# Convolution taps, modulation and residual rows tied in order to the chunks of weights

## Chip, cores and metric

The kernel runs on one core of a Trainium2 chip. The metric is device time in microseconds (us) of one execution, as the median of three. PE is the matmul engine (TensorE), DVE the vector engine, ACT the scalar engine, POOL GpSimd, and SP the engine whose queue issues nearly all DMAs. Each engine works through its own instructions in program order and waits on semaphores for the others.

## What is computed

The program runs two blocks of two layers each, in float32. The first block takes x (256 tokens, width 1024) through windowed attention, a gated convolution and two MLPs. The second block, where most of the change lies, works on x and on 256 tokens of context:

```python
for l in range(DEPTH):
    with_ctx = l < DEPTH - 1
    sh1, sc1, g1, sh2, sc2, g2 = jnp.split((jax.nn.silu(c) @ w_mod[l] + b_mod[l])[:, None, :], 6, axis=-1)
    ...
    u = x * (1.0 + sc1) + sh1
    ...
    y, yc = token_mixer(u, uc, rope, w_in[l], ...)
    x = layer_norm(alpha * x + g1 * y, ln1_g[l], ln1_b[l])
    x = layer_norm(alpha * x + g2 * sq_relu_mlp(x * (1.0 + sc2) + sh2, ...), ln2_g[l], ln2_b[l])
```

The token mixer adds three branches under sigmoid gates: a depthwise convolution of 31 taps over 512 channels, an mLSTM in both directions with 4 heads, and a latent attention (MLA). In layer 1 only the 256 tokens of x are wanted at the end, so its queries, convolution and MLP cover those alone (tokens 256 to 511 in the kernel's numbering; 0 to 255 are the context).

## The kernel before

Every matrix product is done in split precision: an operand is cut into a high part and a low part, and three matmuls (high by high, L326; low by high, L327; high by low, L328) take the place of one. `w()` brings one 512 KB chunk of weights (8 tiles of 128x128): SP issues the DMA into `wr`, ACT copies it to the high part `wh` (L320), DVE subtracts for the low part `wl` (L321). `wr`, `wh` and `wl` have four buffers each, so a chunk's `wh` can't be written before the matmuls of the chunk four places earlier are done. One chunk feeds 24 matmuls, over 256 or 512 tokens.

Each engine's order is set ahead of time by a scheduler that plays the program through with priorities. Three devices steer it. `bg` holds generators that are stepped at marked places (`tick`). `queued()` puts a DMA behind the last DMA of weights. `behind()` gives all that it encloses a priority so low that it only fills gaps in the planned order.

Around the change:
- `conv()`: 120 taps of the convolution for each layer (30 taps by 4 channel tiles; L1061), each one DVE operation on 128x512 (layer 0) or 128x256 (layer 1), under `behind()`. They land among the work of the mLSTM heads.
- `mod(l)`: the modulation vectors from `w_mod`, as 48 DMAs of 512 KB (`mr`) with multiply-adds on DVE (`macd`, L842), then a small matmul (L850) and an addition (L854). `mod(1)` is stepped in `bg` during layer 0's MLP.
- `residual()`: alpha*x plus the row gate*bias for each token tile. The row is computed at full width on DVE (L890, L892: 128x1024), then applied (L900, L901: 128x1024).
- `ln()` normalises a token tile (statistics L954 and L955 on DVE, apply half on ACT L969, half on DVE L971). `make_u()` transposes it on PE (L932), applies the modulation (L937 on ACT, L939 on DVE) and splits it into `uh` (L388, ACT) and `ul` (L389, DVE).
- `ml_gates()`: a chain of operations on 36x512 (scans, copies, exponentials; L1112 to L1137) from the first two projection tiles `p1`, `p2` to the gates of the mLSTM, ending in two sets of transposes (L1145). `ml_project()` makes q, k, v, o of a head (`m_q` L1158 on ACT, `m_k` L1163 on DVE, `m_vt` L1168), and L1191 multiplies q by k.
- `tiles()` computes several projection tiles at once, by a list of parts (from k, to k, from token, to token).

## Time and profile before

| | us |
|---|---|
| median of 3 runs (2387.35 to 2390.11) | 2388.19 |
| the profiled execution's own time | 2387.22 |
| its span in the trace | 2385.2 |
| PE busy in the span | 2292.6 |
| DVE busy | 1722.4 |
| ACT busy | 1125.4 |

The span is the profiled time less 2.0 us around it. PE is busy 96% of it. The difference between span and PE's busy time, 92.6 us, is all the time in which PE had nothing to do; the mean granted clock of PE is 0.986 of full speed.

### The profile page before, as it was taken

To read this page: it belongs to the slowest core of one execution; us is meant where nothing else is said; L and a number is where in the kernel's file an instruction comes from. 1 tells how busy PE (TensorE), PEld (TensorE's weight loads), DVE (VectorE), ACT (ScalarE), POOL (GpSimd) and SP (SyncE) were. 2 spreads that over 40 slices of the span, in tenths; PEclk is the share of its full clock that TensorE was granted. 3 is DMA by queue.
4 is the path that set the end of the run, shared out by engine and by line. 5 is a ranking of instruction groups with operands and counts; after the bars stand their busy time and mean duration, and the time that the engine had idled before them with its cause. 6 is when DMAs were issued, how large, how long until landed. Compare 5 with 4: busy or idle time off the path is not lost.

```text
span 2385.2 us, 35271 instructions
## 1 busy us (share of the span) xinstructions
PE 2292.6 (96%) x13784; PEld 1966.7 (82%) x13796; DVE 1722.4 (72%) x2771; ACT 1125.4 (47%) x1718; POOL 64.1 (3%) x72
## 2 busy tenths in 40 slices
PE   8999989999999999999999999999998799998997
PEld 7888868888999888788777787777777699897996
DVE  6787877977666689956644477577788986857557
ACT  5555555554465444443442335343325355644653
POOL 1001100000000000000000000000000000000000
PEclk9999999999999999999999999999998899999999
DMA  5555546865655653222213343465544333345653
GB/s 198 205 188 175 191 134 204 263 217 185 188 177 187 189 175 106 76 78 65 88 54 115 100 148 132 142 194 180 178 140 138 109 108 115 133 152 185 202 186 114
DMA packets 120662, 364.62 MB, mean 153 GB/s; under 512 B 28528, under 2 KB 30320, under 8 KB 120496
## 3 DMA queue, kind: packets, MB, share of 16 engines
q1 hardware_dynamic: 120496, 362.38, 47.3%
q8 instruction: 108, 1.77, 0.3%
q14 instruction: 58, 0.48, 0.1%
HBM read 359.05 MB, written 3.28 MB: 152 GB/s over the span
## 4 chain that ended last, share of the span: by engine, by line
PE 87%; DVE 7%; DMA 3%; issue 1%; ACT 1%; SPq 0%; DVEq 0%; ACTq 0%
PE mm L326 26%; PE mm L327 26%; PE mm L328 26%; DMA mr<-in_w_mod 2%; DVE wl L321 2%; PE mm L1342 1%; PE tp L675 1%; PE mm L1356 1%; PE mm L1233 1%; DVE macd L842 1%; PE tp L850 1%; PE mm L561 1%; DVE cy L1061 1%; ACT wh L320 1%; PE mm L577 1%
## 5 line engine op out<-in xcount | busy, mean ns | idle before, releaser
L320 ACT CAST wh<-wr 128x1024 fp32r<-128x1024 f32 (+1 forms) x544 | 566.6, 1043 | 879.3 <-PE mm L327 491.7
L321 DVE TENSOR_TENSOR wl<-wr,wh 128x1024 fp32r<-128x1024 f32 (+1 forms) x544 | 658.7, 1213 | 361.4 <-ACT wh L320 351.2
L327 PE MATMUL mm<-ul,wh 128*128 128x256 f32 (+1 forms) x2224 | 709.2, 321 | 11.0 <-DVE ul L389 8.2
L328 PE MATMUL mm<-uh,wl 128*128 128x256 f32 (+1 forms) x2224 | 707.9, 320 | 2.9 <-DVE wl L321 2.9
L326 PE MATMUL mm<-uh,wh 128*128 128x256 f32 (+1 forms) x2224 | 703.8, 323 | 4.4 <-ACT m_q L1158 1.5
L327 PEld LDWEIGHTS mm<-ul,wh 128*128 128x128 f32 x2224 | 421.7, 190 | 45.2 <-DVE ul L389 9.2
L326 PEld LDWEIGHTS mm<-uh,wh 128*128 128x128 f32 x2224 | 415.9, 190 | 47.0 <-issue 5.4
L328 PEld LDWEIGHTS mm<-uh,wl 128*128 128x128 f32 x2224 | 421.2, 190 | 36.7 <-DVE wl L321 3.9
L842 DVE SCALAR_TENSOR_TENSOR macd<-mr,silu_c,macd 128x512 f32<-128x512 f32 x336 | 236.7, 745 | 40.0 <-DMA mr<-in_w_mod 30.9
L328 PE MATMUL mm<-wh,hl 128*128 128x512 f32 x640 | 252.4, 395 | 0.0
L327 PE MATMUL mm<-wl,hh 128*128 128x512 f32 x640 | 252.2, 395 | 0.0
L326 PE MATMUL mm<-wh,hh 128*128 128x512 f32 x640 | 251.1, 395 | 0.0
L326 PE MATMUL mm<-wh,uh 128*128 128x256 f32 x576 | 165.6, 291 | 3.0 <-ACT qk L532 2.3
L327 PE MATMUL mm<-wl,uh 128*128 128x256 f32 x576 | 164.7, 288 | 3.0 <-DVE wl L321 3.0
L328 PE MATMUL mm<-wh,ul 128*128 128x256 f32 x576 | 162.7, 285 | 0.1
L327 PEld LDWEIGHTS mm<-wl,hh 128*128 128x128 f32 x640 | 120.3, 188 | 30.6 <-DVE res L752 0.8
L326 PEld LDWEIGHTS mm<-wh,hh 128*128 128x128 f32 x640 | 120.2, 188 | 30.3 <-issue 2.5
L328 PEld LDWEIGHTS mm<-wh,hl 128*128 128x128 f32 x640 | 120.3, 188 | 28.7 <-issue 0.8
L1061 DVE SCALAR_TENSOR_TENSOR cy<-hpad,vecl,cy 128x512 f32<-128x512 f32 (+1 forms) x240 | 136.6, 606 | 0.1
L326 PEld LDWEIGHTS mm<-wh,uh 128*128 128x128 f32 x576 | 108.7, 190 | 8.3 <-ACT qk L532 3.3
L327 PEld LDWEIGHTS mm<-wl,uh 128*128 128x128 f32 x576 | 109.5, 191 | 7.2 <-DVE wl L321 4.0
L328 PEld LDWEIGHTS mm<-wh,ul 128*128 128x128 f32 x576 | 109.0, 190 | 0.7 <-DVE ul L422 0.3
(292 smaller groups left out, 2811.5 us busy)
## 6 DMA issues: line engine op xcount, KB each, us to landing
wr<-in_m SPq DMA_DIRECT2D x128, 512.0 KB
wr<-in_w SPq DMA_DIRECT2D x128, 512.0 KB
wr<-in_w_in SPq DMA_DIRECT2D x116, 512.0 KB
mr<-in_w_mod SPq DMA_DIRECT2D x96, 512.0 KB
...
```

Of the source, the lines that this page charges most:

```text
L320: nc.scalar.copy(hi[:, :n], raw[:, :n])
L321: nc.vector.tensor_tensor(lo[:, :n], raw[:, :n], hi[:, :n].bitcast(F32), ALU.subtract)
L326: mm(out, lh, rh, start=first, stop=False)
L327: mm(out, lh, rl, start=False, stop=False)
L328: mm(out, ll, rh, start=False, stop=last)
L561: mm(scs[hh][:, a:b], qT[hs, g, pr, qs], kT[hs, g, pr, :] if g == 0 else kT[hs, g, pr, qs], start=False, stop=g == 2)
L577: mm(po[hh * 64:hh * 64 + 64, qt * P:qt * P + P], v[:, j, g, h * 64:h * 64 + 64], pt[hh][:, blk * P:blk * P + P], start=blk == 0, stop=blk ...
L675: nc.tensor.transpose(tp[:, b * P:b * P + P], pm[:, b * P:b * P + P], self.ident)
L842: nc.vector.scalar_tensor_tensor(out=a, in0=raw[:, k], scalar=sc, in1=a, op0=ALU.mult, op1=ALU.add)
L850: nc.tensor.matmul(tp[q:q + 32, :], self.cst("ones")[:, 0:32], acc[:, half, v], start=True, stop=True, tile_position=(0, q))
L1061: nc.vector.scalar_tensor_tensor(out=ys[ft], in0=src, scalar=wk, in1=ys[ft], op0=ALU.mult, op1=ALU.add)
L1233: nc.tensor.matmul(pn[:, d * 130:d * 130 + 129], dts[d][:, s, i * P:i * P + P], v[:, s, 0:129], start=s == ks[0], stop=s == ks[-1])
```

## The change

A list `side` of generators is added. `w()` steps the first of them once after each chunk of weights when `side_n` is 1. What such a step issues stands under `pinned()`: its DMAs follow that chunk's DMA on SP, its ACT work follows that chunk's `wh`, its DVE work that chunk's `wl`. So the taps (6 per chunk in layer 0, 3 in layer 1), the modulation of both layers, and the residual rows have fixed places in each engine's order. `mod(1)` now begins after layer 0's MLA. The row gate*bias is computed once, in a layout of 128x8, by `bias_row()`, and kept in DRAM (`gbd`); the residual loads it ready-made. Layer 1 projects four tiles of the convolution for tokens 256 to 511 first, two k at a time (`BY_QUARTERS`), and the two gate tiles after them. The transposes at the end of the gate chain (`turn()`) come after head 0's projections in the program. Beside these, tiles are put into other pools, `row` has 5 buffers for 6, and layer 0's w_out input has its low half cut into pieces.

```diff
+BY_QUARTERS = tuple((k, k + 2, 256, 512) for k in range(0, 8, 2))
+TAPS = (6, 3)
...
-MT = ((1, 1), (5, 5), (0, 2))
+MT = ((1, 1), (5, 5), (0, 0))
...
+    def spin(self, n):
+        for _ in range(n):
+            if self.side:
+                try:
+                    next(self.side[0])
+                except StopIteration:
+                    self.side.pop(0)
+    def drain_side(self):
+        while self.side:
+            self.spin(1)
+    @contextmanager
+    def pinned(self):
+        with self.tc.issue_after(self.last_w), self.tc.issue_after(self.last_hi), self.tc.issue_after(self.last_lo):
+            yield
...
-        nc.scalar.copy(hi[:, :n], raw[:, :n])
-        nc.vector.tensor_tensor(lo[:, :n], raw[:, :n], hi[:, :n].bitcast(F32), ALU.subtract)
+        self.last_hi = nc.scalar.copy(hi[:, :n], raw[:, :n]).ins
+        self.last_lo = nc.vector.tensor_tensor(lo[:, :n], raw[:, :n], hi[:, :n].bitcast(F32), ALU.subtract).ins
+        self.spin(self.side_n)
...
+            if hc == 0 and bias is not None:
+                self.side_n = 1
...
-                    with self.queued():
+                    with self.pinned():
+                        raw = self.t(self.mp, [P, 2, 512], "mr", bufs=self.nmr)
                         nc.sync.dma_start(raw, self.A[f"w_mod_{l}"][sec * 2 + half, c])
...
+            if sec % 3 == 2:
+                with self.pinned():
+                    self.bias_row(l, sec // 3)
+                yield
...
+    def bias_row(self, l, sub):
+        nc = self.nc
+        row = lambda n: self.A["rows"][n].rearrange("(p k) -> p k", k=KT)
+        prev = l * 6 + 1 if sub else (l - 1) * 6 + 4
+        c = self.t(self.xp, [P, 4, KT], "brow")
+        nc.sync.dma_start(c[:, 2], row(l * 6 + sub * 3))
+        if prev > 0:
+            nc.sync.dma_start(c[:, 3], row(prev + 1))
+        for v in range(2):
+            nc.sync.dma_start(c[:, v], self.gdr[l][v, sub * 3 + 2, :].rearrange("(p k) -> p k", k=KT))
+        for v in range(2):
+            nc.vector.tensor_tensor(c[:, v], c[:, v], c[:, 2], ALU.mult)
+            if prev > 0:
+                nc.vector.scalar_tensor_tensor(out=c[:, v], in0=c[:, 3], scalar=ALPHA, in1=c[:, v], op0=ALU.mult, op1=ALU.add)
+            nc.sync.dma_start(self.gbd[l][v, sub, :].rearrange("(p k) -> p k", k=KT), c[:, v])
...
+    def residual_step(self, r, ag, gb):
+        e = self.nc.vector
+        if ag is None:
+            e.scalar_tensor_tensor(out=r, in0=r, scalar=ALPHA, in1=gb, op0=ALU.mult, op1=ALU.add)
+        else:
+            e.scalar_tensor_tensor(out=r, in0=r, scalar=ALPHA, in1=ag, op0=ALU.mult, op1=ALU.mult)
+            e.tensor_tensor(r, r, gb, ALU.add)
...
+    def residual(self, l, toks, G):
+        ss = sorted({j // 2 for j in toks})
+        with self.pinned():
+            ag = self.row(self.A["rows"][l * 6 + 1:l * 6 + 2])
+            gb = {s: self.row(self.gbd[l][1 - s:2 - s, 1, :]) for s in ss}
+        yield
+        for j in toks:
+            with self.pinned():
+                self.residual_step(self.res[j], ag, gb[j // 2])
...
-        with self.behind():
+        ys = [y[:, ft, :].rearrange("p (s t) -> p s t", s=ns) for ft in range(4)]
+        with self.pinned():
             for ft in range(4):
                 nc.scalar.activation(ys[ft], hp[ft][:, :, 0:256], AF.Identity, scale=self.vecl(f"w_dw_{l}", ft), bias=self.vecl(f"b_dw_{l}", ft))
-            for k in range(1, 31):
-                for ft in range(4):
+        yield
+        taps = [(k, ft) for k in range(1, 31) for ft in range(4)]
+        for a in range(0, 120, TAPS[l]):
+            with self.pinned():
+                for k, ft in taps[a:a + TAPS[l]]:
                     src, wk = hp[ft][:, :, k:k + 256], self.vecl(f"w_dw_{l}", k * 4 + ft)
                     nc.vector.scalar_tensor_tensor(out=ys[ft], in0=src, scalar=wk, in1=ys[ft], op0=ALU.mult, op1=ALU.add)
+            yield
...
+        def turn():
+            with self.tc.issue_after(self.last_mm):
+                for i, src in enumerate((an, li)):
+                    tp = self.ps("tp")
+                    for j in range(4):
+                        nc.tensor.transpose(tp[:, j * R:j * R + R], src[:, j * P:j * P + P], self.ident[0:R, 0:R])
+                    nc.vector.tensor_copy(cl[:, i], tp[:, 0:4 * R].rearrange("p (j r) -> p j r", j=4))
...
-                tis = [0, 1, T_CONV, T_CONV + 1]
-                p1, p2, *pre = self.tiles([A[f"w_in_{l}"][ti, 0] for ti in tis], uh, ul, 0, 512,
-                                           ((0, KT, 0, 256), (0, KT, 256, 512)) if l == 0 else
-                                           ((0, KT, 256, 512), (0, KT, 0, 256, (0, 1))))
-                if l:
-                    pre = [p_[:, 256:512] for p_ in pre]
+                first = lambda tis, c0, parts: self.tiles([A[f"w_in_{l}"][ti, 0] for ti in tis], uh, ul, c0, 512, parts)
+                hp, pre = [], []
+                conv_in = self.conv_in(l, xg, uh, ul, pre, hp)
+                if l == 0:
+                    p1, p2, *more = first([0, 1, T_CONV, T_CONV + 1], 0, ((0, KT, 0, 256), *BY_QUARTERS))
+                    pre += more
+                else:
+                    pre += first(range(T_CONV, T_CONV + 4), 256, BY_QUARTERS)
+                    next(conv_in)
+                    p1, p2 = first([0, 1], 0, ((0, KT, 256, 512), (0, KT, 0, 256)))
...
-                self.conv(l, self.conv_in(l, xg, uh, ul, pre), cy)
+                self.run(conv_in)
+            self.side, self.side_n = [self.conv(l, hp, cy)] + ([self.residual_x()] if l else []), 1
...
+            gates[2]()
...
         if l == 0:
+            self.drain_side()
             hx.close()
...
                 o = self.mla(l, xo, v, ks, qs, cq[0][2])
+                if l == 0:
+                    self.mp, self.nmr = self.cm.enter_context(tc.tile_pool(name="mod1", bufs=1, side="right")), 2
+                    self.side.append(self.mod(1))
...
-            with self.behind():
-                G = self.residual(l, 1, toks, l * 6 + 1)
+            G = {}
+            self.side.insert(0, self.residual(l, toks, G))
...
-                     ((0, KT, 256, 512), (0, KT, 0, 256)) if l == 0 else ((0, KT, 256, 512),), MT[2], ready)
-            self.drain_bg()
+                     (*BY_QUARTERS, (0, KT, 0, 256)) if l == 0 else BY_QUARTERS, MT[2], ready)
+            self.side_n = 0
```

What this makes of the engines' orders is shown at three places. The numbers at a tile's end tell one buffer from another.

First, DVE at the start of layer 0's MLP, while PE waits for `ul`. Before, in the middle of it:

```order
L939 TENSOR_SCALAR mt_13618<-tp_13613,aff_a_13241,aff_b_13242 128x256
L939 TENSOR_SCALAR mt_13628<-tp_13623,aff_a_13241,aff_b_13242 128x256
L890 TENSOR_TENSOR row_13666<-row_13664,row_13658 128x1024
L842 SCALAR_TENSOR_TENSOR macd_13993<-mr_14074,silu_c_83,macd_13993 128x512 x2
L389 TENSOR_TENSOR ul_13240<-mt_13618,uh_13239 128x2x256
L900 SCALAR_TENSOR_TENSOR resb_2291_13210<-resb_2291_13210,row_13660 128x1024
L900 SCALAR_TENSOR_TENSOR resb_2292_13211<-resb_2292_13211,row_13660 128x1024
L389 TENSOR_TENSOR ul_13240<-mt_13628,uh_13239 128x2x256
L892 SCALAR_TENSOR_TENSOR row_13666<-row_13662,row_13666 128x1024
L842 SCALAR_TENSOR_TENSOR macd_13993<-mr_14074,silu_c_83,macd_13993 128x512 x2
L939 TENSOR_SCALAR mt_13638<-tp_13633,aff_a_13241,aff_b_13242 128x256
L890 TENSOR_TENSOR row_13675<-row_13673,row_13658 128x1024
```

After, from the last four `mt` on (L998 and L413 are the former L939 and L389, L344 the former L321, L931 the former L900):

```order
L998 TENSOR_SCALAR mt_13768<-tp_13763,aff_a_13391,aff_b_13392 128x256
L998 TENSOR_SCALAR mt_13778<-tp_13773,aff_a_13391,aff_b_13392 128x256
L413 TENSOR_TENSOR ul_13390<-mt_13768,uh_13389 128x2x256
L413 TENSOR_TENSOR ul_13390<-mt_13778,uh_13389 128x2x256
L998 TENSOR_SCALAR mt_13788<-tp_13783,aff_a_13391,aff_b_13392 128x256
L998 TENSOR_SCALAR mt_13798<-tp_13793,aff_a_13391,aff_b_13392 128x256
L413 TENSOR_TENSOR ul_13390<-mt_13788,uh_13389 128x2x256
L413 TENSOR_TENSOR ul_13390<-mt_13798,uh_13389 128x2x256
L344 TENSOR_TENSOR wl_14054<-wr_14051,wh_14053 128x1024
L344 TENSOR_TENSOR wl_14090<-wr_14087,wh_14089 128x1024
L931 SCALAR_TENSOR_TENSOR resb_2314_13359<-resb_2314_13359,row_14057 128x1024
```

The full-width rows L890, L892, L900, L901 and the `macd` no longer stand between `mt` and `ul`; the residual follows after two chunks' `wl`.

Second, DVE at the end of layer 0's MLP, where the statistics of token tiles 2 and 3 (`resb` ..93 and ..94, the first to be normalised) are made. Before, these rows stand between the last additions of the tiles and their statistics' end:

```order
L321 TENSOR_TENSOR wl_16624<-wr_16621,wh_16623 128x1024
L1574 TENSOR_TENSOR tl_16311<-mm_16229,row_13673 128x512
L954 BN_STATS bst_16359<-resb_2294_13213 128x6
L1577 TENSOR_TENSOR resb_2293_13212<-resb_2293_13212,tl_16308 128x512
L1577 TENSOR_TENSOR resb_2294_13213<-resb_2294_13213,tl_16311 128x512
L321 TENSOR_TENSOR wl_16655<-wr_16652,wh_16654 128x1024
L954 BN_STATS bst_16347<-resb_2293_13212 128x6
L1574 TENSOR_TENSOR tl_16461<-mm_16409,row_13664 128x512
L954 BN_STATS bst_16359<-resb_2294_13213 128x6
L1574 TENSOR_TENSOR tl_16464<-mm_16410,row_13664 128x512
L321 TENSOR_TENSOR wl_16686<-wr_16683,wh_16685 128x1024
L955 BN_AGGR bmv_16345<-bst_16347 128x2
```

After (L1658 and L1661 are the former L1574 and L1577, L1013 and L1014 the former L954 and L955, L1030 the former L971; tiles 2 and 3 are `resb` ..16 and ..17):

```order
L1658 TENSOR_TENSOR tl_16362<-mm_16282,row_14240 128x512
L1661 TENSOR_TENSOR resb_2316_13361<-resb_2316_13361,tl_16362 128x512
L1658 TENSOR_TENSOR tl_16365<-mm_16283,row_14240 128x512
L1013 BN_STATS bst_16382<-resb_2316_13361 128x6
L1661 TENSOR_TENSOR resb_2317_13362<-resb_2317_13362,tl_16365 128x512
L1014 BN_AGGR bmv_16380<-bst_16382 128x2
L1013 BN_STATS bst_16394<-resb_2317_13362 128x6
L387 TENSOR_SCALAR brs_16381<-bmv_16380 128x1
L1014 BN_AGGR bmv_16392<-bst_16394 128x2
L387 TENSOR_SCALAR brs_16393<-bmv_16392 128x1
L1024 TENSOR_SCALAR bmr_16388<-bmv_16380,brs_16381 128x1
L1030 TENSOR_SCALAR resb_2316_13361<-resb_2316_13361,bmv_16380,brs_16381 128x512
```

The `wl` of the next chunks and the `tl` of the other two token tiles have moved behind the normalisation of tiles 2 and 3.

Third, DVE in layer 1 ahead of head 0's `m_k`, for which q by k waits. After:

```order
L1198 COPY g_z_16863<-g_li_16862 4x512
L1122 SCALAR_TENSOR_TENSOR cy_16585<-hpad_16742,vecl_16368,cy_16585 128x256
L1198 COPY g_l_16870<-g_u_16869 4x512
L344 TENSOR_TENSOR wl_17366<-wr_17363,wh_17365 128x1024
L1122 SCALAR_TENSOR_TENSOR cy_16585<-hpad_16993,vecl_16368,cy_16585 128x256
L1122 SCALAR_TENSOR_TENSOR cy_16585<-hpad_17028,vecl_16368,cy_16585 128x256
L1122 SCALAR_TENSOR_TENSOR cy_16585<-hpad_16738,vecl_16368,cy_16585 128x256
L1199 COPY g_li_16862<-g_2863_16860 36x512
L1267 TENSOR_TENSOR g_t_17221<-g_m_17219,trir_16592 128x256
L1200 COPY g_li_16862<-g_2863_16860 4x512
L1229 TENSOR_SCALAR m_k_17080<-mm_17079,vecl_16368 128x512
```

And PE there: before, the gates' transposes L1145 stand ahead of q by k (L1191):

```order
L328 MATMUL mm_17264<-uh_16343,wl_17269 128x256
L1145 MATMUL tp_16801<-cst_65,g_z_16769 128x36 x4
L1145 MATMUL tp_16807<-cst_65,g_li_16768 128x36 x4
L1171 MATMUL tp_17258<-cst_65,m_vt_17226 128x128 x4
L1191 MATMUL mm_17299<-m_q_17160,m_k_17193 128x256
```

After, q by k (L1257) follows the last projection, and the transposes (L1211) follow it:

```order
L352 MATMUL mm_17157<-uh_16378,wl_17162 128x256
L1257 MATMUL mm_17207<-m_q_17043,m_k_17080 128x256
L1257 MATMUL mm_17210<-m_q_17043,m_k_17080 128x256
L1257 MATMUL mm_17213<-m_q_17043,m_k_17080 128x256
L1257 MATMUL mm_17216<-m_q_17043,m_k_17080 128x256
L1237 MATMUL tp_17151<-cst_65,m_vt_17116 128x128 x4
L1211 MATMUL tp_17194<-cst_65,g_z_16863 128x36 x4
```

The gates' transposes have moved behind q by k. `m_k` stands on DVE behind `wl_17366`, the low part of a chunk of head 1 that is four chunks after the one (`wl_17162`) that the last projection of head 0 reads; before, too, it stood behind the `wl` of that chunk, and behind the gate chain.

## Rows read from the trace of the kernel before

**Rows 1.** The page's part 1: busy time, share of the span, instructions.

```profile
PE 2292.6 (96%) x13784; PEld 1966.7 (82%) x13796; DVE 1722.4 (72%) x2771; ACT 1125.4 (47%) x1718; POOL 64.1 (3%) x72
```

**Rows 2.** Waits of PE: line, what ended it, us in total, times, longest.

```profile
PE tp L932 <- ACT resb L969: 17.0, 3, 9.3
PE mm L327 <- DVE ul L389: 8.2, 5, 4.4
```

**Rows 3.** Windows: length; busy PE, PEld, DVE, ACT, POOL; granted clock; DMA share; GB/s.

```profile
0.00:800.00 800.00, 769.32 (x5437) 690.84 (x5450) 600.62 (x862) 434.83 (x656) 39.02 (x24) 0.99 0.60 193
870.00:1010.00 140.00, 137.80 (x658) 110.97 (x658) 138.02 (x261) 56.97 (x109) 3.03 (x4) 1.00 0.30 95
2170.00:2200.00 30.00, 21.81 (x126) 19.21 (x126) 21.45 (x34) 10.75 (x15) 1.29 (x2) 0.83 0.56 193
```

**Rows 4.** Two windows in layer 0's MLP start, columns as in rows 3.

```profile
1440.00:1445.00 5.00, 1.10 (x8) 0.69 (x6) 5.00 (x7) 1.24 (x2) 0.00 (x0) 0.86 0.00 0
1445.00:1450.00 5.00, 3.58 (x16) 3.58 (x17) 5.00 (x8) 0.00 (x0) 0.00 (x0) 0.50 0.00 0
```

**Rows 5.** DVE timeline there: start, us, line, operation, idle before and releaser.

```profile
1440.50 1.22 DVE L890 TENSOR_TENSOR row<-row,row 128x1024 f32<-128x1024 f32 x1
1441.64 0.54 DVE L939 TENSOR_SCALAR mt<-tp,aff_a,aff_b 128x256 f32<-128x256 f32 x1
1442.09 2.35 DVE L901 TENSOR_TENSOR resb<-resb,row 128x1024 f32<-128x1024 f32 x2
1444.36 1.41 DVE L842 SCALAR_TENSOR_TENSOR macd<-mr,silu_c,macd 128x512 f32<-128x512 f32 x2
1445.68 0.69 DVE L389 TENSOR_TENSOR ul<-mt,uh 128x512 fp32r<-128x512 f32 x1
```

**Rows 6.** PE timeline, end of layer 0's MLP and start of layer 1.

```profile
1799.54 0.40 PE L328 MATMUL mm<-wh,hl 128*128 128x512 f32 x1
1809.28 0.69 PE L932 MATMUL tp<-cst,resb 128*128 128x128 f32 x2 [9.34 <-ACT resb L969]
...
1815.23 0.41 PE L327 MATMUL mm<-ul,wh 128*128 128x256 f32 x1
...
1823.54 0.39 PE L327 MATMUL mm<-ul,wh 128*128 128x256 f32 x1 [1.36 <-DVE ul L389]
```

**Rows 7.** DVE timeline at the same boundary.

```profile
1790.94 0.69 DVE L854 SCALAR_TENSOR_TENSOR mt<-tp,mt 128x512 f32<-128x512 f32 x1 [2.61 <-PE tp L850]
...
1803.18 1.22 DVE L321 TENSOR_TENSOR wl<-wr,wh 128x1024 fp32r<-128x1024 f32 x1
```

**Rows 8.** PE timeline, layer 1, last projection of head 0 to q by k.

```profile
1866.51 0.29 PE L326 MATMUL mm<-uh,wh 128*128 128x256 f32 x1
...
1869.28 0.29 PE L328 MATMUL mm<-uh,wl 128*128 128x256 f32 x1
1876.77 0.64 PE L1145 MATMUL tp<-cst,g_z 36*128 36x36 f32 x4 [7.21 <-DVE g_z L1135]
1881.62 0.64 PE L1145 MATMUL tp<-cst,g_li 36*128 36x36 f32 x4 [4.21 <-DVE g_li L1137]
1883.50 1.08 PE L1171 MATMUL tp<-cst,m_vt 128*128 128x128 f32 x4 [1.24 <-ACT m_vt L1168]
1884.87 3.22 PE L1191 MATMUL mm<-m_q,m_k 128*128 128x256 f32 x8 [0.28 <-DVE m_k L1163]
...
1939.72 1.89 PE L1191 MATMUL mm<-m_q,m_k 128*128 128x256 f32 x8
```

**Rows 9.** DVE groups by form: count, busy us, mean ns, idle before.

```profile
L1061 DVE SCALAR_TENSOR_TENSOR cy<-hpad,vecl,cy 128x512 f32<-128x512 f32 x120 | 84.8, 740 | 0.0
L1061 DVE SCALAR_TENSOR_TENSOR cy<-hpad,vecl,cy 128x256 f32<-128x256 f32 x120 | 51.8, 473 | 0.1
```

**Rows 10.** Waits of DVE, columns as in rows 2.

```profile
DVE wl L321 <- ACT wh L320: 351.2, 255, 5.5
DVE macd L842 <- DMA mr<-in_w_mod: 30.9, 23, 3.7
```

155 lines of the change are left out of this document (76 added, 79 removed).

## Prediction

> **What bounds the kernel now.** First the busy times: PE works for 2292.6 of 2385.2 us [rows 1], so whatever the change does to DVE, ACT or the DMAs, it pays only through the 92.6 us in which PE stands idle, or through PE's clock. The same number of matmuls is issued before and after. Next, the waits of PE, to see who owns that idle time: the largest entry is the transposes of `make_u` behind the layer norm (17.0 us in three waits), then matmuls behind `ul` (8.2 us in five) [rows 2]. Last, the timelines at those places. Three stretches hold what the change can touch.
>
> Place A is the start of layer 0's MLP. Two windows of 5 us have PE busy 1.10 and 3.58 us, the second at a granted clock of 0.50, the lower of the two levels (1.2 of 2.4 GHz) [rows 4]. DVE is full there and does other things between `mt` and `ul`: a row (1.22), two residual additions (2.35), two `macd` (1.41) [rows 5].
>
> Place B is the boundary of the layers. The last matmul of the MLP ends at 1799.94; PE then idles 9.34 us, and the first matmul that needs `ul` starts at 1815.23, 15.3 us after that end; another 1.36 us are lost at 1823.54 [rows 6]. DVE reached this late: it had stood 2.61 us at the end of the modulation (L854), and `wl` of later chunks ran among the statistics [rows 7].
>
> Place C is layer 1's first head. Its last projection (24 matmuls, 1866.51 to 1869.57) is followed by waits of 7.21, 4.21, 1.24 and 0.28 us, for the end of the gate chain above all. q by k starts at 1884.87, 15.3 us after the projection's end, and runs 3.22 us, where the same eight elsewhere take 1.89 [rows 8].
>
> **The change part by part.** *A.* The rows, additions and `macd` leave the space between `mt` and `ul`, which becomes 0.54+0.54 and 0.69+0.69 us of DVE work a pair. PE's two windows were 10 us with 4.68 busy: 5.3 us idle, which is to go; of the 3.58 busy at half clock, half, 1.8 us, comes back with it [rows 4]. That is 7.1. A little more is in the other waits for `ul`: the 8.2 less the longest (4.4) less B's 1.36 is 2.4 over three places [rows 2, 6], of which I take 0.5 here: **7.5 us**, from 5.3 (the clock falls anyway, since the layer norm just ahead stays) to 9.5.
>
> *B.* The program now normalises token tiles 2 and 3 without `wl` among the statistics, and without the modulation's end, so that the first transposes come before the MLP's last eight matmuls. After the last matmul DVE has still to do, ahead of the first `ul`: a `tl` and an addition of the last tiles, a statistic (each 512 wide, near 0.69 like the `ul` [rows 5]), a `wl` (1.22 [rows 7]), two `mt` (1.08), another addition, and the `ul` itself: 5 x 0.69 + 1.22 + 1.08 = 5.75 us. So the first `ul` is late by 5.8 us where it was by 15.3: 9.5 us. The following `ul` come every 3 us at most and feed quarters of 24 matmuls, 2.9 to 3.1 us each (24 matmuls of 256 columns, [rows 8]), so 1.36 goes too, less half a us for order: **10 us**, from 7 (layer norm as late as ACT and DVE can make it) to 11.
>
> *C.* The work from the boundary to the end of head 0's last projection is the same; conv tiles go first. What then gates q by k is `m_k`. On DVE it stands behind the `wl` of a chunk whose `wh` buffer is the one that the last projection reads. So after that projection's end come, in series: `wh` on ACT (about 1.05, bounded by the `wl` of the same size, 1.22 [rows 7]), `wl` (1.22), three taps (0.42 each by their pace, 0.47 by their mean [rows 9]), three short copies (0.4 each), `m_k` (0.74, the size of a tap of 512 [rows 9]): 1.05+1.22+1.35+1.2+0.74 = 5.6 us. That is the new wait, in place of 15.3; but the transposes of gates and v (0.64+0.64+1.08 = 2.36 at low clock, about 1.2 at full [rows 8]) were within the 15.3 and now follow q by k as work. 15.3-5.6-1.2 = **8.5 us**, from 4 to 14 (no wait at all, and q by k back to 1.89). The gate chain has to end some 19 us (10+8.5) earlier than it did, with four conv tiles ahead of it and fewer taps between its steps; the sum holds if it ends by `m_k`.
>
> Here a rule speaks against the change. Every matmul, `m_k` and `wl` in the rows ran in the order of its program: nothing overtook `m_q` or `m_k` in the 15.3 us [rows 8]. The Trainium skill, in "TensorE: Matmul & The Clock Gate", section "Architectural detail: the array is 16× 32×32, not 1× 128×128", states that ScalarE and VectorE take their queues strictly first in, first out, and that PE pulls only weight loads ahead. By it C keeps the new wait, and tying work to chunks lengthens every queue behind a late chunk; were it not so, C would give 5.6 us more. The trace agrees with the rule.
>
> *D.* Layer 1's MLP start: 8.2 us of 30 idle [rows 3], 7.2 of it the layer norm's latency (17.0 less 9.34 and small change [rows 2, 6]). That chain is not shortened. The row's load and 0.6 us of `ul` waits go: **1 us**, 0 to 2.
>
> *Modulation in the first block.* The same 124 `macd` and the same DMAs, now at fixed places. Its waits for `mr` (30.9 us in 23, [rows 10]) stand on DVE; PE waits little for weights, and has 30.7 us idle in 800 for all causes [rows 3]. Each waiting `macd` now holds the next chunk's `wl`; four buffers, some 12 us of matmuls at 256 columns, cover the longest wait, 3.7. I take 0, from +3 to -6 (two longest waits reaching PE).
>
> *Layer 0's taps and heads.* 120 taps at 84.8 us [rows 9] in a stretch where DVE is busy 138.02 of 140 and PE 137.80 [rows 3]. Six per chunk spread them over 20 chunks; the load is the same and has no reserve. 0, from +2 to -8.
>
> *The rest.* Six rows and four additions less at 1.22 [rows 5] take 12 us off DVE, mostly in A and B, counted there. `bias_row` adds some 14 operations of 128x8, bounded from below by nothing and from above by 0.54 (a 128x256 [rows 5]): 0 to 7.6 us on a DVE that idles 28% of the span [rows 1], and not on the path. `mod(1)`, 48 portions of four `macd`, 3 us each by 1.41 for two, stands beside MLP chunks of twice 2.9 us: hidden; without that cover each portion would cost its 3 us. 0, +-2.
>
> Sum: 7.5+10+8.5+1 = 27 us. Against the profiled execution's own 2387.2 that is 2360.2; the median of the runs shown is 1.0 above the profiled one, so the forecast is **2361 us**.
>
> **The rivals.** *Less at C.* The gate chain, steps on DVE and ACT in turn, starts later behind conv tiles and is cut by taps, so that it is late again and holds q by k (through ACT, where `m_q` follows its last exponential) or the transposes just behind. For it: it was the longest wait, 7.21+4.21 [rows 8]. Against it: fewer taps stand between its steps. C then gives 0 and the sum is 18.5: about 2370.
>
> *More.* The queues come through without the wait at C and without low clock: 5.6+1.3 us more, and 3 in the first block: about 2351.
>
> *Slower: the tied portions starve the weights.* A `wl` waits for its `wh` 1.38 us on average (351.2 in 255, [rows 10]); now this idle time is filled by taps that may run at any time. Tied taps can't fill it, since they stand behind that very `wl`. If that is paid ahead of each of layer 0's 20 portions and ten of layer 1's 40, it is 41 us where DVE has 2 us of reserve [rows 3]: 2361+41 = 2402. It decides from 20 such portions on, 27 us. Against it: `wl` waits because it is early, four chunks ahead; a DVE that is behind doesn't wait for `wh`. By the Trainium skill's rule above, first in, first out, this is what would happen wherever `wh` itself is late.
>
> *No effect.* The layer norm's latency rules B as it does D, A is held by the same latency, and C's wait only moves: gains of 3 to 5 us and as much lost in the heads: 2387.
>
> **How the numbers follow.** A measurement here can tell about 0.2%, 4.8 us, from no change. Forecast 0.60 (2354 to 2368 by its own bounds), less at C 0.16, more 0.10, slower 0.08, no effect 0.06. Faster by over 0.2% (under 2383.4): the first three, 0.86; same 0.06; slower 0.08. The range leaves out the last two and a little of the case "more": 2348 to 2380.
>
> **What would show it.** Right: in the window of place A PE busy throughout and clock 1.00; at the boundary an idle gap of about 6 us in place of 9.34 and later waits; a wait of PE of 5 to 6 us for `m_k` or `m_q` behind the last projection, and none of over 2 us for the gates; `macd` gone from the layer 0 MLP's end. Wrong: DVE waiting on `wh` between portions of taps with PE waiting for `wl` in the heads of layer 0 (about 870 to 1010), `macd` waits that show up on PE in the first block, or a gate chain that ends after `m_k`.

## The result and the profile after

The changed kernel takes 2359.68 us (median of four runs, 2358.84 to 2359.88) where the kernel before takes 2387.77: a ratio of 0.9881 with a 95% interval of 0.9864 to 0.9898, or 28 us less. The profiled execution has a span of 2357.0 us, 28.2 less than before. The forecast was 2361 us.

The page's part 1 shows something that the forecast did not have. This is the row that answers to [rows 1]:

```profile
PE 2273.7 (96%) x13784; PEld 1965.6 (83%) x13796; DVE 1710.3 (73%) x2779; ACT 1126.6 (48%) x1718; POOL 69.0 (3%) x72
```

PE issues the same 13784 instructions, but its busy time fell by 18.9 us, from 2292.6. Its idle time, the only thing that the prediction counted on, fell by 9.3 us alone (from 92.6 to 2357.0 - 2273.7 = 83.3). So two things have to be explained: where two thirds of the gain come from, and why the idle time that was predicted to go by 27 went by 9.

The waits of PE show where the idle time now stands (us in total, times, longest), against [rows 2]:

```profile
PE mm L1257 <- DMA g_m<-g_md: 7.7, 1, 7.7
PE tp L991 <- ACT resb L1028: 7.2, 1, 7.2
PE mm L1134 <- DVE mt L1132: 7.2, 1, 7.2
PE tp L441 <- DMA x<-in_x_p: 6.1, 1, 6.1
PE mm L409 <- ACT l_h L412: 6.1, 1, 6.1
PE tp L991 <- DVE mt L998: 5.2, 3, 3.3
...
PE mm L1257 <- ACT m_st L1258: 2.8, 4, 1.0
```

The 17.0 us behind the layer norm are down to 7.2 (place D, which stays). The gates' 7.2 and 4.2 are gone, and a 7.7 has come at q by k (L1257), near the forecast's 5 to 6. Two long waits are new: L409, in layer 1's latents, and L1134, the convolution's norm.

Windows of the changed kernel (length; busy PE, PEld, DVE, ACT, POOL; granted clock of PE; DMA share; GB/s):

```profile
0.00:800.00 800.00, 776.93 (x5523) 698.06 (x5536) 607.50 (x873) 441.77 (x662) 40.24 (x25) 0.99 0.60 197
870.00:1010.00 140.00, 134.16 (x643) 107.66 (x641) 136.84 (x269) 61.32 (x124) 3.02 (x4) 1.00 0.29 94
1400.00:1455.00 55.00, 51.93 (x334) 46.77 (x334) 40.21 (x53) 32.57 (x44) 2.16 (x2) 1.00 0.48 163
1600.00:1700.00 100.00, 100.00 (x448) 80.95 (x447) 66.15 (x88) 34.56 (x38) 0.00 (x0) 1.00 0.45 145
1900.00:2060.00 160.00, 144.30 (x1009) 128.88 (x1007) 129.76 (x293) 80.06 (x145) 6.41 (x5) 0.95 0.35 113
```

The first 800 us hold 7.6 us more of busy PE than in [rows 3]. Place A now lies within 1400 to 1455 and keeps its full clock, where [rows 4] had 0.86 and 0.50. The last window, layer 1's latents and the convolution's norm, is the worst: 15.7 of 160 us idle.

The timeline of PE at the boundary, at q by k of layer 1's first head, and at the two new waits:

```profile
1766.25 0.38 PE L991 MATMUL tp<-cst,resb 128*128 128x128 f32 x2
...
1768.10 0.39 PE L352 MATMUL mm<-wh,hl 128*128 128x512 f32 x1
1768.33 0.82 PE L991 MATMUL tp<-cst,resb 128*128 128x128 f32 x6
1772.44 1.82 PE L991 MATMUL tp<-cst,resb 128*128 128x128 f32 x8 [3.29 <-DVE mt L998]
...
1774.91 0.41 PE L351 MATMUL mm<-ul,wh 128*128 128x256 f32 x1
...
1827.77 0.28 PE L352 MATMUL mm<-uh,wl 128*128 128x256 f32 x1
1835.71 3.75 PE L1257 MATMUL mm<-m_q,m_k 128*128 128x256 f32 x8 [7.66 <-DMA g_m<-g_md]
...
1954.59 1.84 PE L409 MATMUL mm<-cst,l_a 128*128 128x1 f32 x8 [6.09 <-ACT l_h L412]
...
2018.20 1.22 PE L1134 MATMUL mm<-mt,cst 128*128 128x256 f32 x2 [7.17 <-DVE mt L1132]
```

At the boundary the first two transposes run between the MLP's last matmuls, as the order said they could, and the first `ul` matmul starts 6.4 us after the MLP's end (1768.49 to 1774.91) where it was 15.3 [rows 6]. At q by k the releaser named, a DMA of `g_m`, is not an operand of the matmul; `m_k` and `m_q` are. DVE ends `m_k` at 1835.40, 0.3 us before, and ACT ends `m_q` at 1835.16, after an idle time that ended with L1200, the last operation of the gate chain on DVE:

```profile
1834.69 0.47 ACT L1224 ACTIVATE m_q<-mm,vecl 128x256 f32<-128x256 f32 x1 [5.64 <-DVE g_li L1200]
```

The timeline of DVE ahead of it:

```profile
1831.09 1.23 DVE L344 TENSOR_TENSOR wl<-wr,wh 128x1024 fp32r<-128x1024 f32 x1
1832.23 1.27 DVE L1122 SCALAR_TENSOR_TENSOR cy<-hpad,vecl,cy 128x256 f32<-128x256 f32 x3
1833.42 0.41 DVE L1199 COPY g_li<-g 36x512 f32<-36x512 f32 x1
1833.75 0.41 DVE L1267 TENSOR_TENSOR g_t<-g_m,trir 128x256 f32<-128x256 f32 x1
1834.20 0.42 DVE L1200 COPY g_li<-g 4x512 f32<-4x512 f32 x1
1834.65 0.75 DVE L1229 TENSOR_SCALAR m_k<-mm,vecl 128x512 f32<-128x512 f32 x1
```

From its `wl` on, that is the series of the prediction (a `wl`, three taps, three short operations, `m_k`), and it is dense: nothing in it waits for `wh`. ACT had ended the `wh` of that `wl` at 1829.05, 2.0 us before DVE came to it.

### The profile page after: what moved, and what is told of

Its sections match the earlier page's. It is cut to its first block, busy times and chain, and to the rows that moved or that the text cites. A ratio compares the mean times of both kernels' runs of the same rounds, so it can differ in the third digit from the quotient of the medians.

```text
span 2357.0 us, 35325 instructions
## 1 busy us (share of the span) xinstructions
PE 2273.7 (96%) x13784; PEld 1965.6 (83%) x13796; DVE 1710.3 (73%) x2779; ACT 1126.6 (48%) x1718; POOL 69.0 (3%) x72
## 4 chain that ended last, share of the span: by engine, by line
PE 52%; DVE 4%; ACT 1%; issue 1%; DMA 0%; POOL 0%; DVEq 0%; ACTq 0%; POOLq 0%
PE mm L350 16%; PE mm L351 15%; PE mm L352 15%; PE mm L1408 1%; DVE wl L344 1%; PE mm L1422 1%; PE mm L1299 1%; PE tp L699 1%; DVE cy L1122 1%; PE mm L1257 1%; PE tp L877 0%; PE tp L991 0%; ACT wh L343 0%; DVE bst L1013 0%; DVE tl L1658 0%
## 5 line engine op out<-in xcount | busy, mean ns | idle before, releaser
L344 DVE TENSOR_TENSOR wl<-wr,wh 128x1024 fp32r<-128x1024 f32 (+1 forms) x544 | 659.7, 1215 | 343.2 <-ACT wh L343 337.6
L352 PE MATMUL mm<-uh,wl 128*128 128x256 f32 (+1 forms) x2224 | 704.8, 319 | 2.7 <-DVE wl L344 2.7
L350 PE MATMUL mm<-uh,wh 128*128 128x256 f32 (+1 forms) x2224 | 701.3, 321 | 4.1 <-ACT m_q L1224 1.5
L350 PEld LDWEIGHTS mm<-uh,wh 128*128 128x128 f32 x2224 | 417.8, 191 | 42.4 <-ACT wh L343 5.0
L352 PEld LDWEIGHTS mm<-uh,wl 128*128 128x128 f32 x2224 | 422.7, 190 | 34.6 <-DVE wl L344 3.7
L352 PE MATMUL mm<-wh,hl 128*128 128x512 f32 x640 | 249.2, 391 | 0.0
L350 PE MATMUL mm<-wh,hh 128*128 128x512 f32 x640 | 247.5, 391 | 0.0
L350 PE MATMUL mm<-wh,uh 128*128 128x256 f32 x576 | 165.4, 291 | 2.6 <-ACT qk L556 1.5
L352 PE MATMUL mm<-wh,ul 128*128 128x256 f32 x576 | 162.9, 285 | 0.1
L350 PEld LDWEIGHTS mm<-wh,hh 128*128 128x128 f32 x640 | 120.0, 188 | 28.3 <-issue 3.4
L352 PEld LDWEIGHTS mm<-wh,hl 128*128 128x128 f32 x640 | 120.1, 188 | 26.7 <-issue 0.8
L350 PEld LDWEIGHTS mm<-wh,uh 128*128 128x128 f32 x576 | 108.4, 190 | 9.6 <-issue 4.6
L352 PEld LDWEIGHTS mm<-wh,ul 128*128 128x128 f32 x576 | 109.0, 190 | 0.7 <-DVE ul L446 0.3
```

What stands on the lines that cost most here:

```text
L344: self.last_lo = nc.vector.tensor_tensor(lo[:, :n], raw[:, :n], hi[:, :n].bitcast(F32), ALU.subtract).ins
L350: mm(out, lh, rh, start=first, stop=False)
L352: self.last_mm = mm(out, ll, rh, start=False, stop=last).ins
```

## Where the 28 us lie, stage by stage

The 11,760 matmuls of the projections (L326 to L328, now L350 to L352) are the same in number in all versions. Numbered in the order in which they start, the start of the same number in two traces says how far one is ahead, and the difference over a stage what the stage gives. Two pairs of kernels are compared, each with its big operands at the same places in SBUF (why that matters is the first experiment): the change against `before_m128`, and `pad128` against the kernel before. Negative is faster, in us.

| stage | after - before_m128 | pad128 - before |
|---|---|---|
| first block, to 518 us | -6.1 | -8.2 |
| from there to layer 0's heads | -1.9 | -1.2 |
| layer 0's heads | +5.2 | +5.4 |
| the end of layer 0's mixers, up to place A | +6.4 | +6.6 |
| place A | -11.0 | -11.1 |
| layer 0's MLP | -1.2 | -1.9 |
| B, the boundary | -12.3 | -12.8 |
| layer 1 to its first heads (C) | -6.9 | -7.0 |
| layer 1's heads | -0.3 | -0.4 |
| layer 1's latents and convolution norm | +21.0 | +22.6 |
| the rest | -1.6 | -0.4 |
| sum | -8.7 | -8.4 |

Most of the +6 ahead of A is moved work: 16 of the small matmuls of `mod(1)` (L877, 605 ns each, 5.2 us busy) run there and no longer at A, in the MLP and at its end (there 8 of them took 3.1 us). Taking it out, A gives about 10 us and B about 9.

## Experiments

The theory, as the two traces suggest it: the edits gain about 30 us at the places predicted and lose 21 in layer 1, because taps at three per chunk end too late; and the change of 18.9 us in busy time is no work of the order at all, but comes from where the tiles lie. The rival: the tied order itself makes PE's pace better. Ratios are against the kernel before, run beside each on the same chip (medians of 2387.08 to 2388.09).

**Placement.** `bias_row`'s small tile takes 128 bytes of each partition, and what is allocated after it in that stack of pools lies 128 bytes elsewhere. In the built programs `uh`, `ul` of the MLP and `hh`, `hl` start 192 bytes past a multiple of 256 before, and 64 past after (`wh` and `wl` 64 in both). Three kernels test it. `pad128` is the change with an unused tile of 128 bytes more, so that these starts are those of before; `pad256` has 256 bytes, so that they stay as in the change. Neither moves any other instruction. This is `pad128`; `pad256` has 64 for 32:

```diff
+            nc.vector.memset(self.t(self.xp, [P, 32], "pad"), 0.0)
```

> As the changed kernel, with one more tile of 128 bytes a partition, written once and never read, so that all tiles opened later lie 128 bytes further on, as far from multiples of 256 bytes as before the change. Theory: layer 0's MLP runs a matmul of 512 columns each 227 ns in the changed kernel and each 232 ns in the kernel before because uh, ul, hh and hl lie elsewhere (64 after, 192 before, past a multiple of 256 bytes); then this kernel's MLP goes back to 232 ns, some 1500 matmuls by 5 ns or 6 to 8 us, and it takes 2364 to 2372. Rival: the pace comes from the multiply-adds and DMAs that stood beside the MLP, or from the chip that ran: no change, 2357 to 2362.

> As the changed kernel, with an unused tile of 256 bytes a partition where the padded kernel had 128. Theory: what counts is the start within 256 bytes, which 256 does not change: 2358 to 2362. Rival: any shift away from where the tiles lie costs, or it is the distance to the weights' tiles: 2365 or more.

And `before_m128` is the kernel before, in its own order, with two tiny tiles (of `rs` and `mr` in the layer norm) merged, which lowers the later tiles by 128 bytes:

```diff
-        rs = self.t(self.xp, [P, 1], "brs", bufs=4)
+        two = self.two = self.t(self.xp, [P, 2], "brs", bufs=4)
+        rs = two[:, 0:1]
...
-            mr = self.t(self.xp, [P, 1], "bmr", bufs=4)
+            mr = self.two[:, 1:2]
```

> The kernel before, with one edit: two of the layer norm's one-column statistics share a tile, which takes 128 bytes a partition less, so that all tiles opened later lie 128 bytes lower: uh, ul, hh and hl of layer 0's MLP then start 64 bytes past a multiple of 256, as in the changed kernel, and not 192. Every engine's order is that of before. Theory: the place of the tiles alone sets the pace of matmuls of 512 columns (227 or 232 ns), and some 16 to 19 of the changed kernel's 28 us are this: 2368 to 2373, with all the waits of before. Rival: the padded kernel was slower for another reason (its tiles meet others, or the change's edits are needed too): 2385 to 2390.

Measured: `pad128` 2378.89 us, ratio 0.9960 (0.9948 to 0.9973), 19.2 us slower than the change and more than expected. `pad256` 2360.83, ratio 0.9890 (0.9877 to 0.9904), no different from the change. `before_m128` 2370.35, ratio 0.9929 (0.9917 to 0.9942): 16.7 us come from placement without any of the change. One window of 100 us in layer 0's MLP, in which PE is busy throughout at full clock and runs little but matmuls of 512 columns, shows how. First the kernel before, then `pad128`, then `before_m128` (the change's own row is above, x448):

```profile
1600.00:1700.00 100.00, 100.00 (x437) 78.93 (x436) 73.20 (x95) 37.72 (x44) 0.00 (x0) 1.00 0.57 181
```

```profile
1600.00:1700.00 100.00, 100.00 (x437) 79.00 (x436) 67.94 (x90) 37.82 (x44) 0.00 (x0) 1.00 0.51 159
```

```profile
1600.00:1700.00 100.00, 100.00 (x448) 80.97 (x447) 77.99 (x101) 39.06 (x46) 0.00 (x0) 1.00 0.59 188
```

The number in brackets behind PE's busy time is to be read: 437 matmuls in 100 us, one in 229 ns, against 448, one in 223. The order of the engines decides nothing here: old order with new places is fast, new order with old places slow. Busy time of the whole span, in `pad128` and in `before_m128`, says the same (2293.6 and 2273.2, beside 2292.6 and 2273.7 of before and after):

```profile
PE 2293.6 (96%) x13784; PEld 1965.7 (83%) x13796; DVE 1711.4 (72%) x2780; ACT 1126.5 (47%) x1718; POOL 67.7 (3%) x72
```

```profile
PE 2273.2 (96%) x13784; PEld 1967.7 (83%) x13796; DVE 1722.0 (73%) x2771; ACT 1125.5 (48%) x1718; POOL 65.2 (3%) x72
```

So of 28 us, 17 to 19 are placement, and the edits give 2388.08 - 2378.89 = 9.2 at the old places and 2370.35 - 2360.83 = 9.5 at the new ones (`pad256` stands for the change here, since it ran beside `before_m128`).

**Taps.** `free_taps` gives the taps back their freedom in both layers, all else tied:

```diff
-        with self.pinned():
+        with self.behind():
...
-            with self.pinned():
+            with self.behind():
                 for k, ft in taps[a:a + TAPS[l]]:
...
-            self.side, self.side_n = [self.conv(l, hp, cy)] + ([self.residual_x()] if l else []), 1
+            self.run(self.conv(l, hp, cy))
+            self.side, self.side_n = [self.residual_x()] if l else [], 1
```

> As the changed kernel, but the taps of both layers are filler again, as before the change; all else is kept. Theory: the taps' fixed portion of 3 a chunk ends 70 us later in layer 1 (2007 against 1937 us) and costs PE the waits of 6.1, 2.4 and 7.2 us in and behind the latent projections and at the convolution's norm; free, these 15 to 20 us come back, while up to 8 us are lost at q by k of head 0, where free taps stand among the gate chain: 2345 to 2355. Rival: the tied taps are what makes the gate chain end in time, and free taps bring back all of 15 us at q by k and more at the boundary: 2365 to 2375.

Measured: 2349.70 us, ratio 0.9842 (0.9829 to 0.9856), 10 us faster than the change. Its window of layer 1's latents and norm (against 144.30 busy and clock 0.95 above), and its longest wait of PE:

```profile
1900.00:2060.00 160.00, 159.28 (x1136) 142.24 (x1135) 112.38 (x249) 89.67 (x164) 4.78 (x6) 1.00 0.37 116
```

```profile
PE tp L1237 <- ACT m_vt L1234: 19.4, 1, 19.4
```

The +21 is gone from its traces, and 11.3 are lost at C, where taps now stand in the gate chain's way (19.4 us at one transpose). The taps of layer 1 end at 1899 us here, at 1937.5 before, and at 2006.7 in the change. In the change the taps are thus still running when PE has come to the norm that needs them.

`taps_6_6` keeps them tied and doubles layer 1's portion:

```diff
-TAPS = (6, 3)
+TAPS = (6, 6)
```

> As the changed kernel, with 6 taps a chunk in layer 1 too, in place of 3. Theory: the taps end by about 1930 us and no longer stand in the latent projections and the convolution's norm, so that most of the 15.7 us of waits there go; the gate chain has twice the taps between its steps, so that q by k waits 5 to 10 us longer: 2350 to 2358. Rival: the waits in the latent projections come from eight copies on ACT ahead of a chunk's cast and not from the taps; then only the 7.2 at the norm go, and the time is 2358 to 2364.

Measured: 2350.53 us, ratio 0.9844 (0.9830 to 0.9857), as fast as `free_taps`. The wait of the norm is gone and 3.6 of L409's 6.1 are left, so 16.5 of the 21 us return; C costs 6.4 more, a wait ahead of head 0's transposes of v:

```profile
1842.08 1.09 PE L1237 MATMUL tp<-cst,m_vt 128*128 128x128 f32 x4 [13.55 <-ACT m_vt L1234]
```

So most of the loss in layer 1 is the size of the portion, not the tie. The 3.6 us that stay at L409 belong to the recorded rival: eight copies on ACT (L1374, 4.25 us together) stand ahead of the next chunk's cast in this trace as in that of the change.

**The wait at q by k.** In the change the scratch tiles of the gate chain lie in a pool that closes when head 0's begins, and head 0's pool takes over its space: in the built program `m_vt` and `m_sg` lie over scratch tiles, `m_q` and `m_k` over other tiles of the closed pool, and all of them stand behind the chain's last read (L1200). `own_space` puts the four scratch tiles of layer 1's chain into the outer pool, which stays open. The tiles of head 0 then lie 8 KB further on, a multiple of 256 bytes; no other line is edited:

```diff
+        xg = self.xb if l else xg
         zeros = t("g_0")
```

> As the changed kernel, but in layer 1 the four scratch tiles of the gate chain (g_0, g_e, g_u, g_l, 8 KB a partition) lie in the outer pool and no longer in the pool that head 0's m_q, m_k, m_vt and m_sg take over when it closes. Nothing else is edited. Theory: what q by k waits for (7.7 us) is not m_k's place behind a chunk's low part, as the forecast had it, but the space: m_q and m_k may be written only when the gate chain has read its last scratch tile. Then the wait goes, up to 3 us of it may reappear at the gates' transposes behind it, and the kernel takes 2351 to 2356. Rival (the forecast's step): the order on DVE rules, the wait stays 5 to 8 us and the time 2358 to 2361.

Measured: 2350.83 us, ratio 0.9845 (0.9832 to 0.9858), 8.9 us faster than the change; the wait of 7.7 is gone, and by the table's method the gain lies at C. `m_q` comes 15.9 us earlier than in the change and waits for nothing, and the timeline of DVE shows `m_k` in the middle of the chain, 11.7 us earlier:

```profile
1818.77 0.45 ACT L1225 ACTIVATE m_q<-mm,vecl 128x256 f32<-128x256 f32 x1
```


```profile
1822.38 0.67 DVE L1187 SCALAR_TENSOR_TENSOR g_z<-g_z,g_l 36x512 f32<-36x512 f32 x1
1822.99 0.73 DVE L1230 TENSOR_SCALAR m_k<-mm,vecl 128x512 f32<-128x512 f32 x1
1823.65 0.47 DVE L1122 SCALAR_TENSOR_TENSOR cy<-hpad,vecl,cy 128x256 f32<-128x256 f32 x1
1824.04 1.21 DVE L344 TENSOR_TENSOR wl<-wr,wh 128x1024 fp32r<-128x1024 f32 x1
```

So `m_q` and `m_k` stood behind the end of the gate chain in the change because of the space. The prediction had seen the order and named the wrong reason for it. In the kernel before, `m_q` was held by the end of the gates, too, there by their transposes:

```profile
1882.35 0.47 ACT L1158 ACTIVATE m_q<-mm,vecl 128x256 f32<-128x256 f32 x1 [5.75 <-PE tp L1145]
```

`gates_first` undoes the other half of C and projects the gates' tiles first again:

```diff
-                    pre += first(range(T_CONV, T_CONV + 4), 256, BY_QUARTERS)
-                    next(conv_in)
-                    p1, p2 = first([0, 1], 0, ((0, KT, 256, 512), (0, KT, 0, 256)))
+                    p1, p2, *more = first([0, 1, T_CONV, T_CONV + 1], 0, ((0, KT, 256, 512), (0, KT, 0, 256, (0, 1))))
+                    pre += [p_[:, 256:512] for p_ in more]
```

> As the changed kernel, but layer 1 projects the two gate tiles and two of the convolution first, in halves, as before the change. Theory: q by k waits for m_k behind the low part of a chunk of head 1 (7.7 us now), not for the gate chain, so an earlier chain gains nothing there; what is lost is PE's time at the boundary, where the first parts need more of ul at once: 2359 to 2364, with the wait ahead of q by k unchanged at 6 to 8 us. Rival: the order of tiles is what gained at q by k; then the wait there goes back to 12 to 15 us and the kernel takes 2366 to 2370.

Measured: 2364.87 us, ratio 0.9905 (0.9891 to 0.9918), 5 us slower: time and wait (10.12 us) both lie between the theory's and its rival's. The chain's work on `g_e` (L1178) starts 1.7 us earlier than in the change, but its last read ends 3.1 us later (1837.75 for 1834.62), and `m_q` and q by k follow that end here, too:

```profile
1838.11 0.47 ACT L1224 ACTIVATE m_q<-mm,vecl 128x256 f32<-128x256 f32 x1 [7.30 <-DVE g_li L1200]
```

```profile
1839.91 3.45 PE L1257 MATMUL mm<-m_q,m_k 128*128 128x256 f32 x8 [10.12 <-DVE m_sg L394]
```

**The boundary.** `late_mod1` starts `mod(1)` in the MLP again, still tied, with the accumulators freed at its end:

```diff
-MT = ((1, 1), (5, 5), (0, 0))
+MT = ((1, 1), (5, 5), (0, 2))
...
-                if l == 0:
-                    self.mp, self.nmr = self.cm.enter_context(tc.tile_pool(name="mod1", bufs=1, side="right")), 2
-                    self.side.append(self.mod(1))
...
-            if l:
+            if l == 0:
+                self.mp, self.nmr = cx.enter_context(tc.tile_pool(name="mod1", bufs=1)), 2
+                self.bg.append(self.mod(1))
+            else:
...
+                        self.drain_bg()
```

> As the changed kernel, but the modulation of layer 1 is stepped in layer 0's MLP again, two steps a place as before, still tied to the chunk at hand. Theory: at the boundary of the layers its last addition and multiply-adds stand ahead of the layer norm's statistics, so that the idle gap there grows from 3.3 back to 9 or more, and the MLP's start gets multiply-adds between mt and ul again: 2368 to 2376. Rival: the boundary's gain comes from the order of the chunks' low parts and of the layer norm alone; then 2358 to 2363.

Measured: 2371.09 us, ratio 0.9935 (0.9921 to 0.9948), 11.4 us slower. The boundary is back as it was in [rows 6], with 9.23 for 9.34:

```profile
1776.10 0.69 PE L991 MATMUL tp<-cst,resb 128*128 128x128 f32 x2 [9.23 <-ACT resb L1028]
```

By the table's method it loses 12.3 us there and gets 6.0 back where `mod(1)` ran in the change. Both of what the prediction named are back in its DVE timeline, the modulation's end (L880 at 1761.56) and chunks' `wl` among the statistics (L344 at 1763.35, 1766.18 and 1769.70), so the run shows that the boundary hangs on where `mod(1)` runs, and not which of the two weighs more. Place A is as in the change, so A does not need `mod(1)` to be elsewhere.

**The residual and the first block.** `free_resid` takes the pin from the residual's rows and additions; `free_mod0` takes it from the first block's modulation, whose DMAs go back to the free queue:

```diff
-        with self.pinned():
+        with self.behind():
             ag = self.row(self.A["rows"][l * 6 + 1:l * 6 + 2])
...
-            with self.pinned():
+            with self.behind():
                 self.residual_step(self.res[j], ag, gb[j // 2])
...
-            self.side.insert(0, self.residual(l, toks, G))
+            self.run(self.residual(l, toks, G))
```

> As the changed kernel, but the residual at the start of both MLPs is filler again (its rows are still loaded ready-made), in place of fixed steps behind the first chunks. Theory: place A's gain is the residual's and the rows' leaving the space between mt and ul; as filler the eight additions of 1.2 us come back there and PE waits 3 to 6 us more at the start of layer 0's MLP: 2363 to 2368. Rival: the multiply-adds of the modulation and the two full-width rows were what filled that space; both stay away, so no change: 2358 to 2362.

```diff
+        pin = self.pinned if l else self.loose
...
-                    with self.pinned():
+                    with pin():
                         raw = self.t(self.mp, [P, 2, 512], "mr", bufs=self.nmr)
-                        nc.sync.dma_start(raw, self.A[f"w_mod_{l}"][sec * 2 + half, c])
+                        with self.queued():
+                            nc.sync.dma_start(raw, self.A[f"w_mod_{l}"][sec * 2 + half, c])
```

> As the changed kernel, but the modulation of layer 0 in the first block is not tied to the chunks (its DMAs follow the weights' as before the change, its multiply-adds go where the scheduler puts them). Theory: the first block's gain, about 9 us of the changed kernel's 28 that the forecast put at 0, comes from tied multiply-adds standing behind a chunk's low part instead of ahead of attention's own DVE work; then this kernel takes 2367 to 2371 and its first 560 us lose what they gained, in waits of PE for DVE's pm, qk, ul and res. Rival: the gain there comes from something else that the change shifts (tile places, the scheduler's other choices); then it takes 2358 to 2362.

Measured: `free_resid` 2359.95 us, ratio 0.9886 (0.9871 to 0.9901): no change. The eight additions (9.4 us of DVE) do stand between `mt` and `ul` again, and PE's window is that of the change (51.92 us busy for 51.93, full clock):

```profile
1421.69 2.36 DVE L932 TENSOR_TENSOR resb<-resb,row 128x1024 f32<-128x1024 f32 x2 [0.81 <-DMA row<-gbd]
1423.97 0.54 DVE L998 TENSOR_SCALAR mt<-tp,aff_a,aff_b 128x256 f32<-128x256 f32 x1
1424.43 1.46 DVE L413 TENSOR_TENSOR ul<-mt,uh 128x512 fp32r<-128x512 f32 x2
1425.80 0.54 DVE L998 TENSOR_SCALAR mt<-tp,aff_a,aff_b 128x256 f32<-128x256 f32 x1
1426.26 2.35 DVE L931 SCALAR_TENSOR_TENSOR resb<-resb,row 128x1024 f32<-128x1024 f32 x2
```

```profile
1400.00:1455.00 55.00, 51.92 (x333) 46.43 (x332) 47.38 (x65) 33.05 (x45) 2.16 (x2) 1.00 0.57 191
```

So A's gain doesn't come from the additions' having moved. Three edits are left for it, and no run takes them apart: the rows made ready by `bias_row`, the `macd` that come behind a chunk's `wl`, and one that neither the prediction nor a run considers at this place: layer 0's MLP, too, begins its first four tiles by quarters of k (`BY_QUARTERS`, at the end of the diff), so that all four use one piece of `ul` before the next is wanted.

`free_mod0` takes 2362.97 us, ratio 0.9900 (0.9887 to 0.9914), 3.3 us slower than the change and not the 7 to 11 expected. Its runs go from 2360.59 to 2366.62 and its interval overlaps that of the change, so the difference is hardly clear of noise; the profiled run is the longest of the four. By the table's method its first block loses 4 us, and waits for `wl` and `ul` come back on PE there:

```profile
132.41 0.39 PE L355 MATMUL mm<-wl,uh 128*128 128x256 f32 x1 [1.22 <-DVE wl L348]
...
365.06 0.39 PE L355 MATMUL mm<-ul,wh 128*128 128x256 f32 x1 [2.31 <-DVE ul L450]
```

**A version that beats both.** `own_free` has free taps and the gate chain's own space together (the diffs of `free_taps` and `own_space`):

> Free taps (2349.7 us) and the gate chain's scratch in the outer pool together. Theory of the space: the 19.4 us that PE waited at head 0's v with free taps go below 8, and the kernel takes 2336 to 2343, below both kernels of the study. Rival: free taps slow the chain itself, and its transposes hold PE as long as before: 2346 to 2351.

Measured: 2336.68 us (2334.55 to 2338.13), ratio 0.9785 (0.9771 to 0.9798): 23 us faster than the change and 51 faster than before. It is a little more than the two gains added (10.0 + 8.9), since of `free_taps`' 19.4 us at C a wait of 6.6 is left:

```profile
PE tp L1212 <- DVE g_li L1201: 6.6, 1, 6.6
```

`own_free_pad192` moves its tiles by 192 bytes more, so that `uh` and `hh` start at a multiple of 256, to see whether that start is as good as 64:

```diff
+            nc.vector.memset(self.t(self.xp, [P, 48], "pad"), 0.0)
```

> The fastest kernel so far (taps free, the gate chain's scratch in the outer pool, 2336.7 us) with an unused tile of 192 bytes a partition: uh and the hh of three MLPs then start at a multiple of 256 bytes, and the hh of the first block's second MLP, which lay 128 past one, lies 64 past. Theory: starts of 0 and 64 both run at 227 ns, so the first block's second MLP gains 5 ns on its 512-column matmuls, about 2 us, and the rest stays: 2332 to 2336. Rival: 0 is not like 64 and all else slows: 2340 to 2355.

Measured: 2343.03 us, ratio 0.9813 (0.9800 to 0.9826), 6.4 us slower than `own_free`, so the theory was wrong for the starts at 0; only its other half came true (64 for 128 in the first block's second MLP, last section). The same window holds 440 matmuls:

```profile
1600.00:1700.00 100.00, 100.00 (x440) 79.52 (x439) 66.32 (x87) 37.09 (x41) 0.00 (x0) 1.00 0.52 158
```

## Why the prediction was right, and where it wasn't

The number was right to 1.3 us, and that is luck. The sum of 27 us was made of idle time; the edits gave 9 of it, since what they gain at A, B, C and in the first block is mostly lost again in layer 0's heads and layer 1's latents, and placement gave 17 to 19 that no step foresaw.

*A* was predicted at 7.5 us (5.3 to 9.5). The place gives 11.0, of which 1.1 are four small matmuls of `mod(1)` moved off it: 9.9, a little above the upper bound. The clock is 1.00 throughout, as forecast. That the space between `mt` and `ul` is what paid is only argued: `free_resid` fills it with the residual again and loses nothing, and the rows, the `macd` and the quarters on PE were not tried apart.

*B* was right, in place, mechanism and size: `ul` late by 6.4 us where 5.8 was worked out, 9.2 without the moved matmuls where 10 was forecast, and `late_mod1` shows that it hangs on `mod(1)` having left.

*C* was mis-sized by some 2 us and its cause was wrong. The stage gives 6.9 where 8.5 was forecast, because q by k starts 7.66 us after the last projection and not 5.6. The step "on DVE it stands behind the `wl` of a chunk whose `wh` buffer is the one that the last projection reads" fails as the cause: that `wl` had no wait for `wh`, DVE was 2.0 us behind, and both operands, `m_q` on ACT as well as `m_k`, were held by the gate chain's last read, through the space. `own_space` shows it: it takes the wait away. With it C is worth 6.9 + 8.9 = 15.8 us, beyond the 14 that were given for no wait at all. The rival "less at C" had the holder right, the end of the gate chain, "through ACT, where `m_q` follows", and its reason (the order on ACT) and its price wrong: C gives 6.9 us and not 0. The Trainium skill's rule in "TensorE: Matmul & The Clock Gate", section "Architectural detail: the array is 16× 32×32, not 1× 128×128", that VectorE takes its queue strictly in order, holds in the rows of DVE above. The mistake was to look for the reason among the instructions ahead and not in what had put `m_k` behind them.

*D* was right: the 7.2 us stay, and the rest of layer 1 gives 0.4 to 1.6.

*The modulation in the first block* was taken at 0, from a gain of 3 to a loss of 6 (the prediction counts gains as positive, the table above as negative). The block gains 6 to 8 us, beyond that bound. By `free_mod0` some 4 us of it may be the tie, at the edge of noise; the rest is not assigned. *Layer 0's heads*, 0 from a gain of 2 to a loss of 8, lose 5. The new waits of q by k for `m_st` (2.8 us in four, in the waits above) are part of it. They stay in `free_taps` (3.4 us in five), which gets only about 1 us of the 5 back by the table's method, so the tie of the taps is not the main cause; it stays open.

The step that failed outright is one that was not made: the prediction spread layer 1's 120 taps over 40 chunks and never asked where PE would be at the fortieth. Its sum has no term for them; only those of layer 0 are weighed, as an equal load. They ended at 2006.7 us where PE reached the norm that needs them at 2011, with the norm's own DVE work still to do behind chunks' `wl`: 21 us, in waits of 6.1, 2.4 and 7.2 and the half clock behind them. Of the 6.1, 3.6 stay when the taps end earlier (`taps_6_6`). The rival "slower" had the tie as a cost, by another mechanism (`wl` starved) and at other places; of that mechanism no row shows anything.

And the step "whatever the change does to DVE, ACT or the DMAs, it pays only through the 92.6 us in which PE stands idle, or through PE's clock" is wrong as a rule: at nearly the same mean clock (0.988 for 0.986) and the same count, PE's busy time went down by 18.9 us, and by 19.4 in `before_m128` (0.987). The Trainium skill warns in "Perfetto Trace Analysis", in the note on judging how close a kernel is to its limit, that matmul busy time is a bad measure of that, since matmuls are pipelined. The rows agree: 100 us of full busy time held 437 or 448 matmuls.
